# Second FFN of a diffusion layer on one Trainium2 core: a written-out order of steps and units, weight tiles that change places, and some moved mixer passes

## The chip, the cores and the metric

The kernel runs on one core of one Trainium2 chip. The metric is the device time of one execution in microseconds (us). The kernel before takes 2628.71 us, the median of three runs (2627.99 to 2629.0). Its profile is one further execution of 2632.15 us, whose instructions span 2630.2 us.

## The reference

The reference computes one layer of a flow-matching backbone on 256 latent tokens and 256 context tokens of width 2048, all in float32:

```
mod = (silu(c) @ w_mod + b_mod)              # 9 vectors: shift, scale, gate of 3 sub-layers
x  = half_step_ffn(x, mod 0..2, w_ffn1)      # latent and context tokens
h  = rms_norm(x) * (1 + scale) + shift       # adaLN
x += gate * mixer(h)                         # 8 attention heads beside 8 mLSTM heads, then w_out
x  = half_step_ffn(x, mod 6..8, w_ffn2)      # latent tokens alone
out = rms_norm(x, g_final)

def half_step_ffn(x, ...):                   # D_FF = 5632
    a, b = split(adaln(x) @ w_up)
    return x + 0.5 * gate * ((silu(a) * b) @ w_down)
```

## The kernel before

The kernel goes through the first FFN (to about 1320 us), the mixer (to about 1920 us) and the second FFN. Every float32 weight tile arrives by DMA as 128 x 2048 values (1 MB) and is *split* by halves (`split`, lines 118 to 133): ScalarE writes a rounded `hi` half of 1024 columns (L125), VectorE the rest `lo` (L126), and TensorE multiplies three times for each block of 128 rows (`mm3`, L147 to L149). There are four `hi` and four `lo` halves in all, so the splits can run about one tile ahead of TensorE. A framework gives each engine an order of its own from the program's order and its dependencies, and sets the waits; each engine then works through its queue in order. SP's queue issues the plain loads, GpSimd's queue (POOL) issues the loads that add to what a tile holds already (`accum`, L728).

**Second FFN.** The hidden width of 5632 is cut into 11 blocks `n` of 512 columns. Block 0 is made from products prepared in the mixer. Blocks 3 and 10 are made plainly (`up`, two token halves by all of w_up). Blocks 1, 2 and 4 to 9 (`QUADS`) are made by `quad`, which gets the up products of a block with seven products of quarter size in place of eight, from sums of weight tiles and sums of token quarters. A quad is a list `order` of seven blocks (a11, a12, n1, s4, s2, s3, a22) of two steps (`q` = 0, 1) each; a step splits one weight tile and runs 12 matmuls into the accumulators X or Y. The weights of these blocks are sums: two *chained* tiles `chain_` are loaded (`again`, L2114), taken in block a11, then added to in place by `accum` loads; two *third* tiles `ra` are loaded (L2123, at block a12), used in block s4, and enter the chained tile by four half sums on VectorE (`summed_half`, L2073, at the places in `between`); block a12 uses *plain* tiles of the three-deep `raw` pool. After each block a function `use` (`p1`, `c11`, `kept`, `p35`, `c12`, `c22`, `c21`) reads the accumulator, forms Silu(a) * b and puts the product into a list `turn`. `turned()` takes the next one from it, transposes it on TensorE (L2052) and splits the result into `hid2h` and `hid2l` (L2055, L2057); three blocks of these can be held (`N_HID`).

The plain work is a list of *units*: 8 of up(3), 8 each of down(0,1), down(2,3), down(4,5), 8 of up(10) and 8 of down(6,7); a unit loads a tile, splits it and runs 24 matmuls. The last loop of `tile_layer` takes the 48 units in turn and after each as many of the 112 steps of the quads as an even share asks for (two or three). down(8,9), block 10 and the final norm follow. The token quarters' differences (`token_forms`: n1, s2, s4, s3) are made on VectorE beside the first units, in scratch from the `ra` tiles.

**Mixer.** Beside its projections, 128 passes over w_mod run on VectorE (`Beside`, L205), paced by the table `PACE`: pairs of a step count and the number of passes due by then. `N_EARLY` and `N_MIXER` say how many passes may use scratch that other tiles take later. `state` (from L1411) transposes the keys of an mLSTM head on TensorE (L1416), copies them (L1418), and weights the values in four ScalarE instructions (L1422) for the product at L1426. `attention` takes a row maximum (L1684), an exponential on ScalarE (L1688), a reciprocal (L1689), scales the row on ScalarE (L1690), and transposes it on TensorE (L1696).

Of the kernel before, what the change touches and what calls it, by code (L numbers as in the profile page):

```python
# [19 lines left out]
P = 128  # L20
# [16 lines left out]

PACE = (4, 2), (12, 13), (19, 19), (27, 28), (35, 37), (41, 44), (49, 51), (56, 54), (62, 61), (67, 70), (70, 76), (71, 85), (76, 96)
PACE += (83, 102), (87, 109), (91, 118), (94, 130), (97, 144), (101, 152), (107, 163), (110, 170), (128, 181)

# [16 lines left out]
def tile_layer(ctx: ExitStack, tc: tile.TileContext, I: dict, out: bass.AP):  # L57
# [1194 lines left out]
    with ExitStack() as mx:  # L1252
# [30 lines left out]
        mm2 = mm2cm.__enter__()  # L1283
        N_EARLY, N_MIXER = 62, 109

# [126 lines left out]
        def state(h, kTc):  # L1412

            tb = tbank()
            for t in range(2):
                nc.tensor.transpose(tb[:, t * P : (t + 1) * P], kTc[:, t * P : (t + 1) * P], ident)  # L1416
            kn = m1.tile([P, 2, P], F32, tag="kn", name="kn", bufs=1)
            nc.scalar.activation(kn, tb[:, :256].rearrange("p (t d) -> p t d", t=2), AF.Copy)  # L1418
            vw = m1.tile([P, 2, 2, 130], F32, tag="E", name="vw")
            for t in range(2):  # L1420
                for d in range(2):
                    nc.scalar.activation(vw[:, t, d, :], v1[CTX][t][:, h, :], AF.Copy, scale=wg[:, t, d, h : h + 1])  # L1422
            yield
            b = bank()
            for t in range(2):
                nc.tensor.matmul(b[:, :260], kn[:, t, :], vw[:, t, :, :], start=t == 0, stop=t == 1)  # L1426
            nc.scalar.activation(C1[:, h, :, :], b[:, :260].rearrange("p (d c) -> p d c", d=2), AF.Copy)
            yield
# [245 lines left out]
        def attention(kv):  # L1674
            items = [(t, g) for t in range(2) for g in range(4)]
            pr, pT, o = {}, {}, {}
            for i in range(len(items) + 2):
                if i < len(items):
                    t, g = items[i]
                    b = bank()  # L1680
                    qs = [x[:, g, t * P : (t + 1) * P] for x in queries(kv)]
                    mm3(b.rearrange("p (a k) -> p a k", a=2), *qs, *keys[kv], True, True)
                    nm = sm.tile([P, 1], F32, tag="nm", name="nm")
                    nc.vector.tensor_reduce(nm, b, axis=AX.X, op=ALU.max)  # L1684
                    nc.vector.tensor_scalar(nm, nm, -ISQ, None, op0=ALU.mult)
# [3 lines left out]
                    nc.vector.reciprocal(sd, sd)  # L1689
                    nc.scalar.activation(p, p, AF.Copy, scale=sd)  # L1690
                    pr[i] = p
# [234 lines left out]
    with f2x:  # L1926
# [50 lines left out]
        acc2 = f2b.tile([P, 2, D], F32, name="acc2", bufs=1)  # L1977
        chain_ = [f3.tile([P, 2048], F32, tag=f"c{q}", name=f"chain2{q}") for q in range(2)]

# [7 lines left out]
        for q in range(2):  # L1987
            nc.sync.dma_start(chain_[q], part(QUADS[0], 0, q))

# [4 lines left out]
        n1, s4, s2, s3 = ([x[:, 0], x[:, 1]] for x in (forms2[g] for g in ("n1", "s4", "s2", "s3")))  # L1994

        def ra_tile():
            return f2b.tile([P, 2048], F32, tag="ra", name="ra")

        def token_forms():
# [20 lines left out]

            v = ra_tile()[:, :1024].rearrange("p (k c) -> p k c", k=8)
            difference(v, a22, a21)
# [7 lines left out]
            yield  # L2030
            v = ra_tile()[:, :1024].rearrange("p (k c) -> p k c", k=8)
            difference(v, a11, a21)
# [4 lines left out]
        turn = []  # L2037
        summed = set()

        def turned():  # L2040

            if not turn:
                return
            n, t, sa, sign = turn[0]
            if n not in hids:
                if n - 1 not in hids or len(hids) - len(summed) >= N_HID:
                    return
                hids[n] = hid_tiles()
# [15 lines left out]
        def wait_turn(n, t, sa, sign):  # L2064
            turn.append((n, t, sa, sign))
            turn.sort(key=lambda x: x[:2])

# [3 lines left out]
        def quad(n):  # L2071

            add = lambda o, x, y: nc.vector.tensor_tensor(o, x, y, op=ALU.add)  # L2073
            mul = lambda o, x, y: nc.vector.tensor_tensor(o, x, y, op=ALU.mult)
            B, ra, g = {}, {}, {}

# [55 lines left out]
            held = lambda q: chain_[q]  # L2132
            order = (
                (a11, held, "X", True, chained(1, 0), p1),
                (a12, plain, "Y", True, ahead, c11),
                (n1, held, "Y", True, None, kept),
                (s4, lambda q: ra[q], "Y", False, None, p35),
                (s2, held, "X", False, chained(0, 2), c12),
                (s3, lambda q: ra[q], "X", False, None, c22),
                (a22, held, "Y", True, again, c21),  # L2140
            )
            for m, (a, src, dst, fresh, then, use) in enumerate(order):
                for q in range(2):
                    if q == 0 and fresh:
                        B[dst] = psx.tile([P, 512], F32, tag=dst, name=dst)
                    wt = split(src(q))
                    if then:
                        then(q)
                    if (m, q) in between:
                        summed_half(*between[m, q])  # L2150
# [70 lines left out]

        N_UNITS, N_FIRST = 2 * 8 + 4 * 8, 2

# [10 lines left out]
        forms = token_forms()  # L2234
        side, n_side, n_quads = quads(), 0, 14 * len(QUADS)
# [7 lines left out]
        assert u == N_UNITS - 1 and n_side == n_quads  # L2243
        drain(side)
        while turn:
            turned()
        before_final()
# [155 lines left out]
```

## Time and profile before

| what | us |
|---|---|
| median of three runs | 2628.71 |
| profiled execution, its own time | 2632.15 |
| its span, first to last instruction | 2630.2 |
| TensorE matmuls busy (98%) | 2584.3 |
| VectorE busy (82%) | 2159.7 |
| ScalarE busy (55%) | 1433.9 |
| GpSimd busy (8%) | 216.2 |

Busy times of different engines overlap, and so do matmuls, whose ends are modelled. In the tables of waits, "PE tr L2052 <- DVE ca L2074" reads: TensorE, about to transpose on line 2052, stood idle until VectorE had written `ca` on line 2074. PE is TensorE, PEld its weight loads, DVE VectorE, ACT ScalarE, POOL GpSimd, SP the engine that issues the plain loads.

### The profile page before, as it was taken

How to read it: one execution, taken by the hardware profiler on the slowest of the kernel's cores; microseconds unless marked ns; L12 is line 12 of the kernel's file. 1: busy time of each engine (PE TensorE's matmuls, PEld its weight loads, DVE VectorE, ACT ScalarE, POOL GpSimd, SP SyncE). 2: the span in 40 equal slices, each digit the busy share in tenths (PEclk: the TensorE clock that was granted, in tenths of full speed). 3: DMA queues.
4: the chain of work that ended last, by engine and by line, in shares of the span. 5: the costliest groups of instructions: out<-in, count | busy, mean ns of one | idle time of the engine just before them, and what ended most of it. 6: DMA issues, size and time to landing. Idle time of an engine off the chain costs nothing.

```text
span 2630.2 us, 33776 instructions
## 1 busy us (share of the span) xinstructions
PE 2584.3 (98%) x12670; PEld 2142.3 (81%) x12670; DVE 2159.7 (82%) x2832; ACT 1433.9 (55%) x1846; POOL 216.2 (8%) x269
## 2 busy tenths in 40 slices
PE   8999999999999999999999999999999999999998
PEld 5788888888888888888889889878897777777776
DVE  7788888878888788888887889888898878887887
ACT  4454444454454565444463466566576666666663
POOL 0000010100010110001210000220000000000001
PEclk8999999999999999999999999999999999999999
DMA  9989999999999989889977877677678878889876
GB/s 392 354 212 265 284 266 282 255 274 284 281 261 291 262 240 234 226 228 219 229 232 276 315 256 266 220 255 275 238 259 270 254 225 245 248 273 273 245 223 172
DMA packets 127220, 681.01 MB, mean 259 GB/s; under 512 B 14153, under 2 KB 16713, under 8 KB 64977
## 3 DMA queue, kind: packets, MB, share of 16 engines
q1 hardware_dynamic: 98544, 493.25, 50.0%
q0 software_dynamic: 28512, 185.61, 36.1%
q8 instruction: 99, 1.62, 0.2%
q14 instruction: 65, 0.52, 0.1%
HBM read 660.91 MB, written 17.89 MB: 258 GB/s over the span
## 4 chain that ended last, share of the span: by engine, by line
PE 81%; DMA 7%; DVE 6%; issue 3%; ACT 2%; POOL 0%; SPq 0%; ACTq 0%; POOLq 0%; DVEq 0%
PE mm L148 21%; PE mm L149 21%; PE mm L147 20%; DVE lo L126 3%; PE mm L85 2%; DMA chain<-in_w_up2b 2%; PE Y L147 2%; PE Y L148 1%; PE Y L149 1%; ACT hi L125 1%; DMA mraw<-in_w_m 1%; PE tr L148 1%; PE tr L149 1%; PE tr L147 1%; PE X L149 1%
## 5 line engine op out<-in xcount | busy, mean ns | idle before, releaser
L125 ACT ACTIVATE hi<-raw 128x1024 fp32r<-128x1024 f32 (+2 forms) x500 | 517.2, 1040 | 441.8 <-PE mm L149 278.4
L126 DVE TENSOR_TENSOR lo<-raw,hi 128x1024 fp32r<-128x1024 f32 (+2 forms) x488 | 584.4, 1207 | 176.5 <-ACT hi L125 153.7
L125 ACT ACTIVATE hi<-chain 128x1024 fp32r<-128x1024 f32 x368 | 388.1, 1059 | 325.8 <-PE mm L149 185.4
L126 DVE TENSOR_TENSOR lo<-chain,hi 128x1024 fp32r<-128x1024 f32 x368 | 445.4, 1221 | 139.8 <-ACT hi L125 136.1
L147 PE MATMUL mm<-hi,hhi 128*128 128x512 f32 (+3 forms) x1024 | 394.5, 385 | 0.0
L148 PE MATMUL mm<-lo,hhi 128*128 128x512 f32 (+3 forms) x1024 | 387.7, 379 | 0.0
L149 PE MATMUL mm<-hi,hlo 128*128 128x512 f32 (+3 forms) x1024 | 387.4, 378 | 0.0
L205 DVE SCALAR_TENSOR_TENSOR junk<-sraw,cBh 128x1024 fp8e5<-128x1024 f32 x192 | 234.3, 1221 | 22.8 <-DMA sraw<-in_w_mt 20.5
L149 PEld LDWEIGHTS mm<-hi,hlo 128*128 128x128 f32 x1024 | 192.9, 188 | 33.9
L147 PEld LDWEIGHTS mm<-hi,hhi 128*128 128x128 f32 x1024 | 192.9, 188 | 31.4
L148 PEld LDWEIGHTS mm<-lo,hhi 128*128 128x128 f32 x1024 | 193.2, 189 | 30.8
L148 PE MATMUL mm<-lo,hid2h 128*128 128x512 f32 x352 | 138.0, 392 | 2.6 <-DVE lo L126 2.5
L147 PE MATMUL mm<-hi,hid2h 128*128 128x512 f32 x352 | 136.7, 392 | 1.1 <-ACT hi L125 1.1
L149 PE MATMUL mm<-hi,hid2l 128*128 128x512 f32 x352 | 137.2, 390 | 0.0
L205 DVE SCALAR_TENSOR_TENSOR sr<-sr,cBl 128x1024 f32<-128x1024 f32 x85 | 102.5, 1216 | 14.9 <-DMA sr<-in_w_mt 14.8
L728 POOL DMA_DIRECT2D chain<-in_w_up1b x60 | 53.0, 884 | 725.9 <-DVE lo L126 700.5
L147 PE MATMUL mm<-hhi,hi 128*128 128x512 f32 (+1 forms) x288 | 101.2, 351 | 0.0
L148 PE MATMUL mm<-hlo,hi 128*128 128x512 f32 (+1 forms) x288 | 98.9, 343 | 0.0
L149 PE MATMUL mm<-hhi,lo 128*128 128x512 f32 (+1 forms) x288 | 98.9, 343 | 0.0
L125 ACT ACTIVATE hi<-ra 128x1024 fp32r<-128x1024 f32 x64 | 67.9, 1061 | 53.6 <-PE mm L149 31.7
L126 DVE TENSOR_TENSOR lo<-ra,hi 128x1024 fp32r<-128x1024 f32 x64 | 77.5, 1222 | 21.1 <-ACT hi L125 19.6
L148 PEld LDWEIGHTS mm<-lo,hid2h 128*128 128x128 f32 x352 | 66.1, 188 | 18.5 <-DVE lo L126 5.1
(515 smaller groups left out, 5665.6 us busy)
## 6 DMA issues: line engine op xcount, KB each, us to landing
raw<-in_w_dn SPq DMA_DIRECT2D x70, 1024.0 KB, 7.8
chain<-in_w_up1b POOLq DMA_DIRECT2D x60, 1024.0 KB, 10.4
sraw<-in_w_mt SPq DMA_DIRECT2D x96, 512.0 KB, 8.4
sr<-in_w_mt SPq DMA_DIRECT2D x82, 512.0 KB, 5.4
raw<-in_w_up1b SPq DMA_DIRECT2D x40, 1024.0 KB, 8.4
mraw<-in_w_m SPq DMA_DIRECT2D x32, 1024.0 KB, 7.6
raw<-in_w_up2b SPq DMA_DIRECT2D x32, 1024.0 KB, 8.1
chain<-in_w_up2b POOLq DMA_DIRECT2D x32, 1024.0 KB, 11.0
```

Source lines behind the costliest of these rows:

```text
L85: ins = getattr(self.engine, name)(*a, **k)
L125: scalar[0].activation(hi, src, AF.Copy)
L126: vector[0].tensor_tensor(lo, src, hi.bitcast(F32), op=ALU.subtract)
L147: tensor[0].matmul(out_ap, sh, mh, start=first, stop=False, skip_group_check=skip)
L148: tensor[0].matmul(out_ap, sh, ml, start=False, stop=False, skip_group_check=skip)
L149: tensor[0].matmul(out_ap, sl, mh, start=False, stop=last, skip_group_check=skip)
L205: ins = nc.vector.scalar_tensor_tensor(junk() if junk else raw, raw, 1.0, cB[s], op0=ALU.mult, op1=ALU.mult, accum_out=mT[:, i, s, kt, h : ...
L728: accum = lambda dst, src: nc.gpsimd.dma_start(dst, src, accum_op=ALU.add)
```

## The change

1. The last loop no longer shares out steps by a count. A generator `sequence` writes the order: two units, and then for each quad two steps, and six times two steps and a unit (no unit after the fourth block in the last quad of each four).
2. `turned()` takes a product only when two further places of that order (`N_TURN`, counted by `clock`) have gone by since it was formed.
3. The chained and third tiles are two pairs, `weights`, that change roles with each quad. The next quad's first load goes into the third pair at block s3, not into the chained pair at block a22. The third tiles are loaded at block a11 instead of a12.
4. The half sums are put ahead of or behind other splits (`early`, `late_`); each sum and load stays once per quad.
5. The token forms use part of `acc2` as scratch.
6. In the mixer: the table `PACE`, `N_EARLY` (62 to 65) and `N_MIXER` (109 to 111) bring passes forward; in `state` the weighted values come before the transposes, and two of the four move to VectorE; in `attention` the scaling of the row moves to VectorE.

```diff
+N_TURN = 2
-PACE = (4, 2), (12, 13), (19, 19), (27, 28), (35, 37), (41, 44), (49, 51), (56, 54), (62, 61), (67, 70), (70, 76), (71, 85), (76, 96)
-PACE += (83, 102), (87, 109), (91, 118), (94, 130), (97, 144), (101, 152), (107, 163), (110, 170), (128, 181)
+PACE = (4, 2), (12, 13), (19, 19), (27, 28), (35, 37), (42, 44), (51, 51), (58, 54), (65, 61), (70, 70), (73, 76), (74, 85), (79, 96)
+PACE += (86, 102), (92, 109), (98, 118), (100, 130), (103, 144), (106, 152), (109, 163), (112, 170), (128, 181)
...
+            vw = m1.tile([P, 2, 2, 130], F32, tag="E", name="vw")
+            for d in range(2):
+                nc.scalar.activation(vw[:, 0, d, :], v1[CTX][0][:, h, :], AF.Copy, scale=wg[:, 0, d, h : h + 1])
+                nc.vector.tensor_scalar(vw[:, 1, d, :], v1[CTX][1][:, h, :], wg[:, 1, d, h : h + 1], None, op0=ALU.mult)
...
-                    nc.scalar.activation(p, p, AF.Copy, scale=sd)
+                    nc.vector.tensor_scalar(p, p, sd, None, op0=ALU.mult)
...
+            if clock[0] < born[n, t] + N_TURN:
+                return
...
+            i = QUADS.index(n)
+            chain_, ra = weights[i % 2], weights[1 - i % 2]
+
             def again(q):
                 if n != QUADS[-1]:
-                    nc.sync.dma_start(chain_[q], part(QUADS[QUADS.index(n) + 1], 0, q))
+                    nc.sync.dma_start(ra[q], part(QUADS[i + 1], 0, q))
...
-            def ahead(q):
-                ra[q] = ra_tile()
+            def first(q):
+                accum(chain_[q], part(n, 1, q))
                 nc.sync.dma_start(ra[q], part(n, 1, 2 + q))
...
-                if h:
-                    accum(ra[q], part(n, 1, q))
-
-            between = {(2, 1): (0, 0), (3, 0): (0, 1), (3, 1): (1, 0), (4, 0): (1, 1)}
+
+            def early(m, q):
+                if (m, q) == (3, 0):
+                    summed_half(0, 1)
+                elif (m, q) == (4, 0):
+                    summed_half(1, 1)
+                    accum(ra[1], part(n, 1, 1))
+
+            def late_(m, q):
+                if (m, q) == (2, 1):
+                    summed_half(0, 0)
+                elif (m, q) == (3, 0):
+                    accum(ra[0], part(n, 1, 0))
+                elif (m, q) == (3, 1):
+                    summed_half(1, 0)
...
-                (a11, held, "X", True, chained(1, 0), p1),
-                (a12, plain, "Y", True, ahead, c11),
+                (a11, held, "X", True, first, p1),
+                (a12, plain, "Y", True, None, c11),
...
-                (s3, lambda q: ra[q], "X", False, None, c22),
-                (a22, held, "Y", True, again, c21),
+                (s3, lambda q: ra[q], "X", False, again, c22),
+                (a22, held, "Y", True, None, c21),
...
+        def sequence():
+
+            yield from "uu"
+            for n in range(len(QUADS)):
+                yield from "ss"
+                for m in range(1, 7):
+                    yield from "ss"
+                    if m != 3 or n % 4 != 3:
+                        yield "u"
...
-        for u, _ in enumerate(units()):
-            steps(forms)
+        streams = {"u": units(), "s": quads()}
+        for x in sequence():
+            next(streams[x])
+            if x == "u":
+                steps(forms)
+            clock[0] += 1
             turned()
-            while n_side < n_quads * (u + 1 - N_FIRST) / (N_UNITS - N_FIRST):
-                next(side)
-                n_side += 1
-                turned()
```

More of the change, by code (lines that the diff above doesn't have):

```diff
@@ L1283, in tile_layer @@
         mm2 = mm2cm.__enter__()
-        N_EARLY, N_MIXER = 62, 109
+        N_EARLY, N_MIXER = 65, 111
         early2 = one([P, 2, 1024], "early2", tag="mqT")
@@ L1418, in state @@
             nc.scalar.activation(kn, tb[:, :256].rearrange("p (t d) -> p t d", t=2), AF.Copy)
[L1419 to L1422, printed above, removed]
             yield
@@ L1977, in tile_layer @@
         acc2 = f2b.tile([P, 2, D], F32, name="acc2", bufs=1)
-        chain_ = [f3.tile([P, 2048], F32, tag=f"c{q}", name=f"chain2{q}") for q in range(2)]
+        weights = [[f3.tile([P, 2048], F32, tag=f"c{q}", name=f"chain2{q}") for q in range(2)]]
+        weights.append([f2b.tile([P, 2048], F32, name=f"ra{q}", bufs=1) for q in range(2)])
         LAST = NF // FB - 1
@@ L1987, in tile_layer @@
         for q in range(2):
-            nc.sync.dma_start(chain_[q], part(QUADS[0], 0, q))
+            nc.sync.dma_start(weights[0][q], part(QUADS[0], 0, q))
         hv = [x.rearrange("p k (t c) -> p t k c", t=2) for x in (h2hi[:, :, :T], h2lo[:, :, :T])]
@@ L1994, in tile_layer @@
         n1, s4, s2, s3 = ([x[:, 0], x[:, 1]] for x in (forms2[g] for g in ("n1", "s4", "s2", "s3")))
-        def ra_tile():
-            return f2b.tile([P, 2048], F32, tag="ra", name="ra")
         def token_forms():
@@ L2019, in negative_less @@
                 sub(v, v, l)
-            v = ra_tile()[:, :1024].rearrange("p (k c) -> p k c", k=8)
+            v = acc2[:, 0, :1024].rearrange("p (k c) -> p k c", k=8)
             difference(v, a22, a21)
@@ L2030, in token_forms @@
             yield
-            v = ra_tile()[:, :1024].rearrange("p (k c) -> p k c", k=8)
+            v = acc2[:, 0, 1024:].rearrange("p (k c) -> p k c", k=8)
             difference(v, a11, a21)
@@ L2038, in tile_layer @@
         summed = set()
+        born, clock = {}, [0]
         def turned():
@@ L2065, in wait_turn @@
             turn.append((n, t, sa, sign))
+            born[n, t] = clock[0]
             turn.sort(key=lambda x: x[:2])
@@ L2074, in quad @@
             mul = lambda o, x, y: nc.vector.tensor_tensor(o, x, y, op=ALU.mult)
-            B, ra, g = {}, {}, {}
+            B, g = {}, {}
             def p1():
@@ L2145, in quad @@
                         B[dst] = psx.tile([P, 512], F32, tag=dst, name=dst)
+                    early(m, q)
                     wt = split(src(q))
@@ L2148, in quad @@
                         then(q)
-                    if (m, q) in between:
-                        summed_half(*between[m, q])
+                    late_(m, q)
                     for j in range(4):
@@ L2220, in units @@
             yield from down(6, 7)
-        N_UNITS, N_FIRST = 2 * 8 + 4 * 8, 2
+        def sequence():
[6 more added lines that the diff above has]
+                        yield "u"
         def before_final():
@@ L2234, in tile_layer @@
         forms = token_forms()
-        side, n_side, n_quads = quads(), 0, 14 * len(QUADS)
-        for u, _ in enumerate(units()):
-            steps(forms)
-            turned()
-            while n_side < n_quads * (u + 1 - N_FIRST) / (N_UNITS - N_FIRST):
-                next(side)
-                n_side += 1
-                turned()
-        assert u == N_UNITS - 1 and n_side == n_quads
-        drain(side)
+        streams = {"u": units(), "s": quads()}
[4 more added lines that the diff above has]
+            clock[0] += 1
+            turned()
+        for x in streams.values():
+            assert next(x, x) is x
         while turn:
+            clock[0] += 1
             turned()
```

## The prediction

> **What bounds the kernel now.** I read the page first, then a table of stages, then the table of TensorE's waits in the last stage, and only then the timeline around single waits. The stage table (busy us of each engine in each stretch, granted clock, DMA share):
>
> ```profile
> span 2630.2 us, 33776 instructions
> ```
>
> ```profile
> core 0: us, PE busy (x) PEld busy (x) DVE busy (x) ACT busy (x) POOL busy (x), PEclk, DMA share, GB/s
> 400.00:1000.00 600.00, 600.00 (x2702) 495.89 (x2701) 494.45 (x616) 308.08 (x355) 54.64 (x62) 1.00 0.97 270
> 1735.00:1835.00 100.00, 97.04 (x519) 80.78 (x518) 82.97 (x148) 71.17 (x110) 6.51 (x6) 0.98 0.75 267
> 1950.00:2600.00 650.00, 630.79 (x2779) 510.47 (x2778) 517.68 (x492) 398.91 (x422) 47.08 (x54) 1.00 0.85 251
> ```
>
> TensorE is the bound: in the first FFN (400 to 1000) it is never idle. In the second FFN (1950 to 2600) it is idle for 650.0 - 630.8 = 19.2 us, and that is the pool from which the main edit can win. Who ended those waits, by the table of waits of that stretch (us in total, times, longest):
>
> ```profile
> PE tr L2052 <- DVE ca L2074: 6.5, 6, 1.8
> PE mm L148 <- DVE lo L126: 3.8, 6, 0.8
> PE mm L147 <- ACT hi L125: 2.5, 4, 0.8
> PE Y L147 <- DVE ca L2073: 2.2, 3, 0.9
> PE Y L147 <- ACT cy L2087: 2.1, 6, 0.7
> PE X L148 <- DVE lo L126: 1.9, 3, 0.7
> ```
>
> A wait costs more than its idle figure. Two places of TensorE's timeline (start, duration, idle before it in brackets):
>
> ```profile
> 2163.74 0.69 PE L147 MATMUL mm<-hi,hid2h 128*128 128x512 f32 x2
> 2165.10 0.50 PE L148 MATMUL mm<-lo,hid2h 128*128 128x512 f32 x1 [0.68 <-DVE lo L126]
> 2165.43 0.39 PE L149 MATMUL mm<-hi,hid2l 128*128 128x512 f32 x1
> 2165.67 0.39 PE L147 MATMUL mm<-hi,hid2h 128*128 128x512 f32 x1
> ...
> 2184.09 0.39 PE L149 MATMUL mm<-hi,hid2l 128*128 128x512 f32 x1
> 2186.30 0.63 PE L2052 MATMUL tr<-ident,ca 128*128 128x128 f32 x4 [1.82 <-DVE ca L2074]
> ```
>
> Undisturbed matmuls start 0.23 us apart but last 0.39, so 0.16 of each stall is booked as busy (2184.09 to 2186.30 is 2.21, of which 1.98 is lost and 1.82 shown). The first matmul after a wait also takes 0.33 to the next start, 0.10 more. The six rows hold 28 waits and 19.0 us: 6 before transposes lose 6.5 + 6 x 0.16 = 7.5 us, the other 22 lose 12.5 + 22 x 0.26 = 18.2. **Pool: 25.7 us.**
>
> Why VectorE and ScalarE are late there:
>
> ```profile
> ACT hi L125 <- DMA chain<-in_w_up2b: 26.8, 13, 3.9
> ...
> ```
>
> ```profile
> 1950.00:1997.00 47.00, 45.04 (x198) 36.38 (x197) 46.52 (x43) 30.48 (x33) 2.70 (x3) 1.00 0.79 265
> ...
> 2147.00:2222.00 75.00, 71.75 (x315) 57.59 (x314) 60.05 (x59) 45.32 (x48) 5.22 (x6) 1.00 0.84 251
> ```
>
> ScalarE waits 13 times for a chained tile to land. VectorE is busy 60 of 75 us in a typical quad but 46.5 of the first 47 us, where it also makes the token forms.
>
> **The change part by part.** *Fixed order.* A quad has 14 steps of 12 matmuls (2.7 us each) and takes 6 units of 24 matmuls (5.4 us). Before, a counter puts a unit after every second or third step, wherever that falls; TensorE's built order cuts blocks in two and even units ("2 matmuls of a unit, 12 of Y, 22 of the unit"). After, a unit stands behind every block of two steps but the first, so whole blocks of 24 alternate. Every accumulator that a block reuses has then a unit of 5.4 us in which VectorE or ScalarE may read it: the Y waits (2.2 + 2.1 us idle, 9 times) end. No instruction is added; the work of a quad is 14 x 12 + 6 x 24 matmuls on both sides.
>
> VectorE's load per block and unit. Its rows (mean ns) and its back-to-back pace:
>
> ```profile
> L126 DVE TENSOR_TENSOR lo<-chain,hi 128x1024 fp32r<-128x1024 f32 x368 | 445.4, 1221 | 139.8 <-ACT hi L125 136.1
> ...
> L2073 DVE TENSOR_TENSOR chain<-chain,ra 128x1024 f32<-128x1024 f32 x32 | 38.4, 1219 | 0.2
> ```
>
> ```profile
> 1980.84 2.35 DVE L126 TENSOR_TENSOR lo<-chain,hi 128x1024 fp32r<-128x1024 f32 x2
> 1983.11 1.22 DVE L2001 TENSOR_TENSOR s3f<-ra,s3f 128x1024 fp32r<-128x1024 f32 x1
> ```
>
> Two splits start 2.27 apart, so I count 1.14 each (and 0.6 for a 512-wide add of 0.68). Block plus unit needs 6 splits = 6.8 us against 10.9 us of TensorE. The fullest pair (n1) adds two half sums (2.3), one add (0.6) and, in half of the cases, two additions to the output (1.2): 10.9 against 10.9, with the buffers' lead of one step (2.7) as reserve. The two blocks without a unit between them need 9.1 + 1.2 + 0.6 = 10.9 against 10.9, after a unit that needs 2.3 of 5.4. So ordinary quads stall little: I take 1 us for all (0 to 8, the upper end being one wait of about 1 us per quad). The first quad still carries token forms; in the built order of VectorE s4, s3 (15 passes of the four forms in all, 17 us) fall among the half sums of blocks n1 and s4. Walking that queue with 1.14 per pass, from the start of the first unit (the forms begin 0.5 later), five halves come late, in us ready / wanted: the first plain tile's second half 18.0 / 17.7, the unit after n1 33.5 / 33.0, the two tiles of s4 39.3 / 39.0 and 42.6 / 42.0, the unit after s4 46.0 / 45.2. Together 0.3 + 0.5 + 0.3 + 0.6 + 0.8 = 2.5, with resumes 3 us (2 to 6); before, 1.96 us idle there. Where the cover of a unit is gone (blocks s4 and s2 of every fourth quad) VectorE has only splits to do.
>
> *Late turn.* A product may be transposed two places after it is formed, so 5.4 us or more of matmuls lie between the last matmul of a block and its transposes. Add, Silu and product need about 0.7 + 0.6 + 0.7 plus two splits in VectorE's queue, 4.3 us. The 7.5 us go; what is late next is the second half of the hidden block, first read two blocks later, so nothing. At the end 16 transposes instead of 8 stand together before the last products: 0.5 us lost (0 to 1.5).
>
> *Tiles change places.* The next quad's first load goes into the third tile at s3 rather than into the chained tile at a22: 4 steps and 2 units of lead, 21.7 us, in place of 2 steps and at most a unit or two. On SP's queue it stands between the two plain tiles, and waits for splits that are done in that same order, so it holds nothing up. The third tile's load now follows the previous a22. Landing times in the stage:
>
> ```profile
> q0 software_dynamic: 7485, 49.81, 42.3%
> q1 hardware_dynamic: 13894, 101.20, 41.7%
> ...
> chain<-in_w_up2b POOLq DMA_DIRECT2D x30, 1024.0 KB, 11.4
> ...
> chain<-in_w_up2b SPq DMA_DIRECT2D x14, 1024.0 KB, 6.8
> ```
>
> 21.7 covers 6.8 three times, so these ScalarE waits go. Accumulating loads at s4, s2 have 4 steps and 2 units too. The first ones (block a11 to block n1) have 4 steps and one unit, 16.3 us from start to start; less 1.4 (the second half of the split may be that late) and 2.3 (one hi and one lo ahead of the matmul) leaves **12.6 us**, up to 15 where the split ran a step ahead, against the median 11.4. Bandwidth: 84% of 610 us for some 8 quads is 63 us per quad; in 71.5 us that is 0.88, and the first FFN ran 0.97 without a wait.
>
> Sum for the stage: 25.7 - 1 - 3 - 0.5 = **21.2 us** won. The acc2 scratch for the forms adds nothing: nothing else uses it yet.
>
> *Mixer.* Scaling of the attention rows goes from ScalarE to VectorE, half of the weighted values too, and the paced passes come up to 7 places earlier (128 passes on both sides, hidden beside TensorE, as VectorE has 17% idle; a pass without that cover costs 1.14).
>
> ```profile
> PE tr L1696 <- ACT pr L1690: 3.0, 2, 2.1
> ...
> PE tr L1416 <- ACT cy L1458: 0.6, 1, 0.6
> PE mm L1426 <- ACT kn L1418: 0.5, 1, 0.5
> ```
>
> ```profile
> L1690 ACT ACTIVATE pr<-pr,sd 128x512 f32<-128x512 f32 x16 | 11.5, 718 | 5.5 <-DVE sd L1689 5.4
> ...
> L1422 ACT ACTIVATE vw<-v1c,wg 128x130 f32<-128x130 f32 x32 | 10.1, 395 | 0.1
> ```
>
> ```profile
> L2281 DVE TENSOR_SCALAR acc<-acc,rstd 128x512 f32<-128x512 f32 x3 | 1.4, 484 | 0.7 <-POOL rstd L2274 0.7
> ...
> L1909 DVE TENSOR_SCALAR rr<-ones,rstd 128x128 f32<-128x128 f32 x2 | 0.6, 288 | 1.4 <-POOL rstd L155 1.4
> ```
>
> VectorE gets 16 x 0.48 + 16 x 0.29 = 12.4 us, ScalarE loses 11.5 + 6.3. The shown waits are 4.1 us; a shorter path by 0.2 and one hand-over less takes part of them. Bounds: all 4.1 plus the slow clock below (5.8 won), or 5 us lost if VectorE (83% busy) becomes late for splits. I take 2 us won, near the waits' rows.
>
> ```profile
> 1745.03 1.23 DVE L205 SCALAR_TENSOR_TENSOR sr<-sr,cBl 128x1024 f32<-128x1024 f32 x1 [0.52 <-DMA sr<-in_w_mt]
> ...
> 1748.28 0.66 PE L1696 MATMUL tr<-ident,pr 128*128 128x128 f32 x4 [2.07 <-ACT pr L1690]
> ...
> 1749.36 0.66 PE L147 MATMUL mm<-hi,hhi 128*128 128x512 f32 x1
> 1749.82 0.63 PE L148 MATMUL mm<-lo,hhi 128*128 128x512 f32 x1
> ```
>
> After the idle 2.07 us matmuls start 0.46 apart, and the granted clock of that stretch is 0.98: 0.02 x 100 us is some 2 us of lost clock. [...] In my sum the clock stands only as the upper bound.
>
> Sum: 2632.15 (the profiled execution's own time) - 21.2 - 2 = 2609. The median of the runs shown, 2628.71, lies 3.4 below that execution, so **2606 us** is predicted.
>
> **Rivals.** (1) *The chained tile lands late, moderately.* For: third-tile loads may now stand beside the first accumulating loads, 4 MB within two steps. Against: SP issues them behind the a22 splits, a unit earlier. Landing at about 14 us instead of 11.4 costs 1.5 us in each of 8 quads: 2606 + 12 = 2618. [...]
>
> (2) *The same transfer, slower than before.* All landings of the chained tile in the stage:
>
> ```profile
> DMA to landing us min/median/max: 5.5/9.3/17.3
> ```
>
> If each quad met the longest, 17.3 - 12.6 = 4.7 us would be lost in block n1, 8 times: 2606 + 38 = 2644. It ends slower once a landing passes 12.6 + 23/8 = 15.5. For: 17.3 does occur. Against: it occurs where four accumulating loads follow each other, which the first pair does not meet.
>
> (3) *VectorE becomes late in the mixer:* the 5 us above in place of 2 won: 2613.
>
> (4) *The waits only move:* every block of two steps waits for VectorE's half sums as long as before; about 2629. Against: VectorE has 20% idle in the quads.
>
> **Chances.** Forecast 0.60, (1) 0.17, (2) 0.06, (3) 0.10, (4) 0.07. Range: below, the whole pool and the mixer's bound, 2632.15 - 25.7 - 4.5 - 3.4 = 2599; above, rival (1), 2619. A measurement tells about 0.2% (5 us) from no change. Faster 0.87, same 0.07, slower 0.06.
>
> **What would show it.** Right: in the second FFN TensorE idles 3 to 6 us instead of 19.2, no row of transposes waiting for ca, no ScalarE wait for chained loads at a11, remaining waits in the first quad. Wrong: waits of hi for the chained tile at n1 (rivals 1, 2); a new row of transposes or matmuls waiting for VectorE's pr or lo between 1461 and 1835 (rival 3).

## The result, and the profile after

The changed kernel takes 2604.93 us (median of four runs, 2603.34 to 2609.73), the kernel before, timed beside it, 2628.59 us (2627.99 to 2629.0). The ratio is 0.9913 with a 95% interval of 0.9896 to 0.993: 23.7 us faster. The profiled execution took 2604.58 us.

The stage table of the changed kernel (columns as before; the last stretch ends at 2573, where block 10 and the last products begin to run out):

```profile
span 2602.7 us, 33781 instructions
```

```profile
1735.00:1835.00 100.00, 97.31 (x525) 80.93 (x523) 83.84 (x151) 57.45 (x91) 10.38 (x10) 1.00 0.67 228
1950.00:2573.00 623.00, 622.19 (x2775) 512.91 (x2774) 519.71 (x493) 403.60 (x422) 47.21 (x54) 1.00 0.88 261
```

In the second FFN TensorE is idle for 623.0 - 622.2 = 0.8 us, where it was 19.2. Its table of waits there has three rows left, one wait each, and all three lie in the first quad:

```profile
PE Y L150 <- DVE lo L128: 0.3, 1, 0.3
PE mm L150 <- DVE lo L128: 0.3, 1, 0.3
PE Y L149 <- ACT cy L2091: 0.2, 1, 0.2
```

No transpose waits for `ca` any more. ScalarE's waits for loads of the chained tiles in that stretch (26.8 us, 13 times, before) are down to three; the pairs change roles, so the same load bears the name chain in one quad and ra in the next:

```profile
ACT hi L127 <- DMA chain<-in_w_up2b: 4.3, 2, 3.5
...
ACT hi L127 <- DMA ra<-in_w_up2b: 2.2, 1, 2.2
```

In the mixer the longest wait has only changed the engine that ends it: it was ScalarE's `pr`, it is VectorE's, and is as long as before.

```profile
PE tr L1698 <- DVE pr L1692: 2.8, 2, 2.1
...
PE tr L1422 <- ACT cy L1460: 0.7, 1, 0.7
```

**Where the time came from** is seen best by cutting each trace at two instructions of TensorE: the first matmul that reads `h2hi` (the products prepared for block 0, in the last 20 us of the mixer) and the last matmul of all. From TensorE's timeline, the kernel before, then the changed one:

```profile
1901.06 0.37 PE L442 MATMUL mm<-h2hi,hi 128*128 128x258 f32 x1
...
2619.75 0.39 PE L149 MATMUL mm<-hi,hid2l 128*128 128x512 f32 x1
```

```profile
1900.58 0.37 PE L444 MATMUL mm<-h2hi,hi 128*128 128x258 f32 x1
...
2592.97 0.39 PE L151 MATMUL mm<-hi,hid2l 128*128 128x512 f32 x1
```

The stage shrinks from 2619.75 - 1901.06 = 718.7 us to 2592.97 - 1900.58 = 692.4 us, 26.3 us. Everything ahead of it differs by 0.5 us, the tail behind it by 0.7. So in this pair of traces the whole gain is in the second FFN, and the mixer's edits gave about nothing; ffn_only and mixer_only, below, test that.

### The profile page after: what moved, and what is told of

Its sections match the earlier page's. It is cut to its first block, busy times and chain, and to the rows that moved or that the text cites. A ratio compares the mean times of both kernels' runs of the same rounds, so it can differ in the third digit from the quotient of the medians.

```text
span 2602.7 us, 33781 instructions
## 1 busy us (share of the span) xinstructions
PE 2575.7 (99%) x12670; PEld 2144.7 (82%) x12670; DVE 2170.6 (83%) x2864; ACT 1417.7 (54%) x1810; POOL 220.7 (8%) x269
## 4 chain that ended last, share of the span: by engine, by line
PE 85%; DVE 7%; DMA 5%; issue 2%; ACT 1%; POOL 0%; ACTq 0%; POOLq 0%; SPq 0%; DVEq 0%
PE mm L151 21%; PE mm L150 21%; PE mm L149 21%; DVE lo L128 2%; PE mm L87 2%; PE Y L149 2%; PE Y L151 2%; PE Y L150 2%; PE X L151 2%; PE X L150 2%; PE X L149 2%; PE tr L150 1%; PE tr L149 1%; PE tr L151 1%; PE tr L87 1%
## 5 line engine op out<-in xcount | busy, mean ns | idle before, releaser
L127 ACT ACTIVATE hi<-chain 128x1024 fp32r<-128x1024 f32 x336 | 355.0, 1059 | 305.7 <-PE mm L151 188.0
L128 DVE TENSOR_TENSOR lo<-chain,hi 128x1024 fp32r<-128x1024 f32 x336 | 407.2, 1221 | 118.0 <-ACT hi L127 114.3
L207 DVE SCALAR_TENSOR_TENSOR junk<-sraw,cBh 128x1024 fp8e5<-128x1024 f32 x192 | 234.3, 1220 | 19.2 <-DMA sraw<-in_w_mt 16.7
L128 DVE TENSOR_TENSOR lo<-ra,hi 128x1024 fp32r<-128x1024 f32 x96 | 117.0, 1223 | 39.7 <-ACT hi L127 35.8
L127 ACT ACTIVATE hi<-ra 128x1024 fp32r<-128x1024 f32 x96 | 101.9, 1061 | 65.1 <-PE mm L151 48.4
L149 PE MATMUL mm<-hi,sumshl 128*128 128x512 f32 x200 | 77.8, 389 | 0.0
```

The costliest lines, as they stand in the source:

```text
L127: scalar[0].activation(hi, src, AF.Copy)
L128: vector[0].tensor_tensor(lo, src, hi.bitcast(F32), op=ALU.subtract)
L149: tensor[0].matmul(out_ap, sh, mh, start=first, stop=False, skip_group_check=skip)
L207: ins = nc.vector.scalar_tensor_tensor(junk() if junk else raw, raw, 1.0, cB[s], op0=ALU.mult, op1=ALU.mult, accum_out=mT[:, i, s, kt, h : ...
```

## The experiments

Three groups of four kernels; the kernel before was timed again beside each group (2632.75, 2631.86 and 2630.83 us), so the ratios compare, not the times. "Stage" is the time between the two matmuls above in the kernel's one trace, "idle" what TensorE idles from 1950 to 2573 (in held_first, whose stage ends 85 us later, this is a smaller part of the work).

| kernel | us | ratio and 95% interval | stage | idle |
|---|---|---|---|---|
| before (first profile) | 2628.59 | 1 | 718.7 | 19.1 |
| order_only | 2615.48 | 0.9933 (0.9921 to 0.9946) | 703.2 | 8.8 |
| tiles_only | 2625.33 | 0.997 (0.9959 to 0.9982) | 707.9 | 10.1 |
| turn_at_once | 2607.27 | 0.9904 (0.9889 to 0.9919) | 692.1 | 0.8 |
| no_swap | 2608.42 | 0.9912 (0.9898 to 0.9925) | 694.9 | 3.8 |
| ffn_only | 2604.06 | 0.9895 (0.9881 to 0.991) | 691.7 | 0.5 |
| mixer_only | 2634.21 | 1.0012 (1.0002 to 1.0021) | 717.2 | 18.7 |
| sums_back | 2608.45 | 0.9908 (0.9893 to 0.9922) | 693.3 | 1.6 |
| late_first | 2605.57 | 0.9895 (0.9879 to 0.9912) | 693.4 | 1.4 |
| turn_only1 | 2631.38 | 0.9999 (0.9989 to 1.0008) | 717.3 | 19.0 |
| held_first | 2693.33 | 1.0236 (1.0219 to 1.0252) | 776.7 | 55.0 |
| best | 2603.08 | 0.9894 (0.9877 to 0.9911) | 691.2 | 0.5 |
| after_again | 2604.42 | 0.9902 (0.9886 to 0.9917) | 691.5 | 0.5 |

The stage is the sharper measure: kernels whose second FFN is that of before lie at 717.2 to 718.7 (mean 717.7), those with the changed one at 691.2 to 692.4 (mean 691.7), while the time ahead of it scatters from 1898.9 to 1907.2 over all these traces (1900.6 and 1907.0 for the very same changed kernel).

### Which part won: the second FFN or the mixer

ffn_only is the changed kernel with the mixer's lines as before; mixer_only is the kernel before with the mixer's lines changed:

```diff
-                    nc.vector.tensor_scalar(p, p, sd, None, op0=ALU.mult)
+                    nc.scalar.activation(p, p, AF.Copy, scale=sd)
... (and PACE, N_EARLY, N_MIXER, vw as before)
```

> The changed kernel with the mixer as before (pace, state, attention). Theory: the mixer edits are worth what the two traces show, waits of 4.1 us idle before against about 4.6 after, so nothing or at most 1 us: 2604 to 2607. Rival (the prediction's term): 2 us, 2607; or the mixer edits cost and this is faster, 2602.

> The kernel before with the mixer edits alone. Theory: within 1 us of the kernel before, 2628. Rival (the prediction's term): 2626.5; rival (VectorE late): 2633.

ffn_only is as fast as the changed kernel, as its theory had it. mixer_only wins nothing, it is slower by 0.5 to 5.5 us: 1.0012 (1.0002 to 1.0021). So of the three expectations for it the rival with VectorE late is nearest, though the interval is wide. Its wait stands at the same place with the same length, now ended by VectorE:

```profile
PE tr L1696 <- DVE pr L1690: 3.2, 2, 2.1
```

Beside it stand two rows of transposes that wait for VectorE (L1604, 0.6 us each). Rows of this kind, 0.8 to 2.3 us together, are in every trace with the mixer's edits and in none without them.

### Order or tiles

order_only puts the written-out sequence into the kernel before and nothing else. tiles_only is the changed kernel with the old share-out by a count and no late turn; the change of roles, the sums' places, the scratch and the mixer's edits stay.

```diff
 order_only (from before)
+        streams = {"u": units(), "s": quads()}
+        for x in sequence():
+            next(streams[x])
+            if x == "u":
+                steps(forms)
             turned()
-            while n_side < n_quads * (u + 1 - N_FIRST) / (N_UNITS - N_FIRST):
...
 tiles_only (from after)
-N_TURN = 2
+N_TURN = 0
+            while n_side < n_quads * (u + 1 - N_FIRST) / (N_UNITS - N_FIRST):
...
```

> The kernel before with the written-out order of steps and units alone (turn at once, old tile roles, old places of the half sums, old mixer). Theory (each of the three FFN edits removes its own waits): the Y waits and most split waits go, the waits of transposes for ca (6.5 us idle) stay, and the chained tile reloaded at a22 has 2 steps and 1 unit, 10.9 us, less 3.7 of lead, so 7 us against landings of 7 to 9: about 1 us of TensorE lost per quad. TensorE idle 10 to 12 us in the second FFN instead of 19.2, time about 2615. Rival A (the order does it all): idle under 2 us, 2606. Rival B (the exchange of the tiles does it): idle over 15, about 2623.

> The changed kernel with the old sharing-out of steps and turn at once: exchange of tiles, new places of the half sums and the mixer edits stay. Theory: ScalarE's waits for chained tiles at a11 go, Y waits and waits of transposes stay: TensorE idle 12 to 15 us in the second FFN, time about 2620. Rival A (order does it all): idle about 19, 2627. Rival B (tiles do it): idle under 6, about 2610.

Against the 717.7 us of the old stage order_only wins 14.5 and tiles_only 9.8; together 24.3, against 26.0 for the whole change. The two are close to additive, and take away different waits. The theory for order_only held, with a little less idle time (8.8 us) than it had. That for tiles_only held in time (2620 expected is 0.997 of before) but not in its reason: the transposes' waits, which it expected to stay, went. TensorE's waits of order_only:

```profile
PE tr L2052 <- DVE ca L2074: 4.4, 4, 3.0
PE X L147 <- ACT s3f L2006: 3.7, 1, 3.7
```

and of tiles_only:

```profile
PE mm L150 <- DVE lo L128: 4.1, 7, 0.8
PE Y L149 <- DVE ca L2077: 2.7, 4, 0.9
PE Y L149 <- ACT cy L2091: 2.1, 6, 0.7
```

The fixed order ends the waits of Y and of `lo`, which tiles_only still has. The tiles end the transposes' waits, which order_only still has, without any late turn. order_only's second row is the s3 form of the first quad: its scratch is a tile of the `ra` pool, and it comes some 25 us later in the stage than in the changed kernel, where the scratch is `acc2`. ScalarE's timeline of order_only, then of the changed kernel:

```profile
2015.52 1.06 ACT L2006 ACTIVATE s3f<-ra 128x1024 fp32r<-128x1024 f32 x1 [1.52 <-DVE ra L2001]
```

```profile
1988.31 1.06 ACT L2006 ACTIVATE s3f<-acc 128x1024 fp32r<-128x1024 f32 x1 [0.76 <-DVE acc L2001]
```

The 3.7 us wait has a second price: behind it the granted clock is 0.50 for 3.4 us, another 1.7 us. The scratch alone was not tried. Every kernel with it in `acc2` lacks that row; but so does the kernel before, which has its scratch in `ra` too and makes this form at 1981.73, ahead of the third tiles' use. So it is that scratch together with the written-out order that is late.

### Why the transposes waited

The prediction had the late turn remove these waits. The rival: the Silu that `ca` needs stands in ScalarE's queue behind a `hi` split that waits for a chained tile to land. ScalarE's timeline of the kernel before around the transposes at 2263 us (which wait 1.5 us):

```profile
2258.24 2.01 ACT L125 ACTIVATE hi<-chain 128x1024 fp32r<-128x1024 f32 x2 [2.72 <-DMA chain<-in_w_up2b]
...
2261.19 0.63 ACT L2105 ACTIVATE ca<-ca 128x512 f32<-128x512 f32 x1 [0.95 <-DVE ca L2073]
...
2263.70 0.60 ACT L2055 ACTIVATE hid2h<-tr 128x512 fp32r<-128x512 f32 x1 [1.88 <-PE tr L2052]
```

The two `hi` halves start 2.7 us late, and the Silu of L2105 (its operand from VectorE, 0.95 us late, hangs on the `lo` of the same tile in VectorE's queue) follows them. That is no single case: each of the six waits of transposes in this trace ends 3.1 to 4.8 us after such a late split of a chained tile began, and so do the four of order_only (4.8 us each). Three kernels tell the two apart: turn_at_once (the changed kernel without the late turn), turn_only1 (the kernel before with a late turn of one place, half of the changed kernel's two; as I read the code, with two the old share-out would reach a hidden block before it is transposed), and no_swap (the changed kernel, late turn and all, but with fixed roles, the next quad's first load at a22 again).

```diff
 turn_at_once
-N_TURN = 2
+N_TURN = 0
 turn_only1 (from before)
+N_TURN = 1
+            if clock[0] < born[n, t] + N_TURN:
+                return
 no_swap
-            chain_, ra = weights[i % 2], weights[1 - i % 2]
+            chain_, ra = weights
...
-                    nc.sync.dma_start(ra[q], part(QUADS[i + 1], 0, q))
+                    nc.sync.dma_start(chain_[q], part(QUADS[i + 1], 0, q))
```

> The changed kernel with N_TURN 0, so that a product may be transposed as soon as it is in the list. Theory: the transposes wait for ca again, 16 turns of which some 6 to 10 wait 1 us: TensorE idle 6 to 9 us in the second FFN, time 2605 + 7 = 2612. Rival: in the fixed order the framework finds a better place for the transposes by itself, idle under 2 us, 2605.

> The changed kernel with fixed roles: the next quad's first load goes into the chained tile again, at a22. Theory: that load has 2 steps and a unit of lead (about 7 us net) against a landing of 7 to 9, ScalarE waits for it at a11 in most quads, TensorE loses about 1 us in each of 7 quads: idle 5 to 8 us, time about 2612. Rival: VectorE's and ScalarE's lead of one tile hides it, idle under 2 us, 2605.

> The kernel before with the late turn alone (one place of the sequence, N_TURN = 1). Theory (transposes wait because ScalarE, which works in order, has the Silu of that block behind a hi split that waits for the chained tile's load): most of the transposes' waits stay, TensorE idles at least 15 of the 19.2 us in the second FFN, the time is 2626 to 2631, ratio 0.999 to 1.001. Rival (the prediction's step: a later turn removes them): no row of transposes waiting for ca, idle about 12.5, 7 us faster, ratio about 0.997.

turn_at_once has the whole gain (stage 692.1), turn_only1 none of it (717.3), and no_swap keeps two waits of transposes in spite of the late turn. The waits go with the loads, in all three, and in tiles_only, which has the loads early, the product turned at once and no such wait. The theory of turn_at_once (transposes wait again, 7 us lost) failed, that of turn_only1 held. turn_only1's row, and the load row beside it:

```profile
PE tr L2057 <- DVE ca L2080: 6.3, 6, 1.6
...
ACT hi L127 <- DMA chain<-in_w_up2b: 20.9, 10, 3.7
```

and no_swap's:

```profile
PE tr L2055 <- DVE ca L2078: 3.3, 2, 1.7
...
ACT hi L127 <- DMA chain<-in_w_up2b: 18.2, 9, 4.1
```

ScalarE still waits 18.2 us in no_swap, and the stage is only 3.2 us longer by it: the fixed order leaves most of these waits covered. The theory for no_swap (about 1 us lost in each of seven quads) was too dark: two quads lost it.

### The leads of the loads

sums_back puts the half sums and the third tile's accumulating loads to their old places. late_first moves the line of the first accumulating load from block a11 to block a12. held_first does that in earnest: GpSimd first reads one column of the plain tile's `lo`, with a small operation whose result nobody uses, and only then issues the load.

```diff
 sums_back
-                    early(m, q)
...
-                    late_(m, q)
+                    if (m, q) in between:
+                        summed_half(*between[m, q])
 late_first
-                accum(chain_[q], part(n, 1, q))
...
-                (a12, plain, "Y", True, None, c11),
+                (a12, plain, "Y", True, chained(1, 0), c11),
 held_first
-                accum(chain_[q], part(n, 1, q))
...
+                    if m == 1:
+                        seen = sm.tile([P, 1], F32, tag="nm", name="seen")
+                        pin(nc.gpsimd.tensor_scalar(seen, wt(slice(CB * 3, CB * 3 + 1))[1].bitcast(F32), 1.0, 0.0, op0=ALU.mult, op1=ALU.add))
+                        pin(accum(chain_[q], part(n, 1, q)))
```

> The changed kernel with the half sums at the places of the kernel before (after their step's split) and each third tile's accumulating load after both its sums. Theory: the built order of VectorE moves the sums anyway and a unit stands beside each pair, so TensorE idle stays under 2.5 us: 2605 to 2607. Rival (their place matters): a wait of about 1 us per quad, 2613.

> The changed kernel with the first accumulating load of each chained tile one block later (at a12 instead of a11), so with 2 steps and a unit of lead instead of 4 steps and a unit: net 12.6 - 5.4 = 7.2 us, up to 9.6 where the split ran ahead, against landings of 8 to 12. Theory (landing beyond the net lead stops TensorE at block n1, the point of rivals 1 and 2): hi at n1 waits for the chained tile in nearly every quad, TensorE loses 1 to 3 us in each of 8 quads, 2613 to 2629. Rival (the lead has more slack than was counted): under 0.5 us per quad, 2605 to 2609.

> The changed kernel; before each first accumulating load GpSimd reads one column of the lo half of the block after a11 (a small operation whose result nobody uses), so the two loads into the chained tiles are issued one block, about 5.4 us, later: net lead 7 us in place of 12.5, against landings of 8 to 10. Theory (the lead of this load is what the kernel lives on, rival 1 of the prediction): ScalarE waits for the chained tile before block n1 in nearly every quad and TensorE stalls there, 1 to 2 us a quad: 2613 to 2621, ratio 0.994 to 0.997. Rival (the splits run far enough ahead that 5 us less of lead are absorbed): under 0.5 us a quad, within 4 us of the changed kernel, ratio 0.990 to 0.993.

sums_back costs some 1.6 us of stage, hardly more than the scatter; its theory held. late_first tests nothing: GpSimd's queue holds few other things, its issue waits only for the `lo` of a11, and so happens at the same time with the line at either place (131.6 us into the stage in the changed kernel, 132.1 here, in the second quad). held_first really moves it. In the changed kernel's second quad GpSimd issues the two loads and ScalarE takes the first of the tiles (it comes under the name ra in this quad):

```profile
2032.16 0.86 POOL L730 DMA_DIRECT2D ra<-in_w_up2b  x1 [26.93 <-DVE lo L128]
...
2037.29 0.88 POOL L730 DMA_DIRECT2D ra<-in_w_up2b  x1 [4.26 <-DVE lo L128]
...
2044.53 1.06 ACT L127 ACTIVATE hi<-ra 128x1024 fp32r<-128x1024 f32 x1 [0.30 <-PE Y L151]
```

The lead (from the issue to the start of the split) is 12.4 us, and ScalarE is held by a buffer that TensorE still reads, not by the load. In held_first:

```profile
2054.13 1.25 POOL L2170 TENSOR_SCALAR seen<-lo 128x1 f32<-128x1 f32 x1 [34.98 <-DVE lo L128]
2055.33 0.89 POOL L730 DMA_DIRECT2D ra<-in_w_up2b  x1
...
2058.30 0.91 POOL L730 DMA_DIRECT2D ra<-in_w_up2b  x1
```

```profile
2067.41 2.00 ACT L127 ACTIVATE hi<-ra 128x1024 fp32r<-128x1024 f32 x2 [9.26 <-DMA ra<-in_w_up2b]
...
2074.73 2.00 ACT L127 ACTIVATE hi<-ra 128x1024 fp32r<-128x1024 f32 x2 [4.80 <-DMA ra<-in_w_up2b]
```

ScalarE wants the first tile at 2067.41 - 9.26 = 2058.2: 2.8 us after its issue, where I meant to leave 7. In the changed kernel the same moment, when ScalarE is free for the split, lies 12.1 us after the issue; so the hold took 9.3 us of lead, not 5.4. The small operation itself is 1.25 us of that; the rest is how far the awaited `lo` lies behind a11's in VectorE's queue. And the two loads, now 3 us apart, are there only 12 and 16 us after their issue. TensorE pays in each quad:

```profile
PE Y L149 <- ACT hi L127: 42.3, 15, 7.0
PE Y L150 <- DVE lo L128: 12.1, 19, 0.8
```

```profile
1950.00:2573.00 623.00, 567.95 (x2404) 455.71 (x2403) 457.25 (x429) 352.03 (x376) 57.21 (x60) 0.96 0.77 230
```

The stage grows by 776.7 - 691.7 = 85.0 us, 10.6 a quad, and the kernel is slower than before, 1.0236 (1.0219 to 1.0252). Up to 2573 the idle time is 55 us; a granted clock of 0.96 is another 0.04 x 623 = 25: behind the 7.04 us wait that ends at 1986.95 and the 3.31 us wait that ends at 2068.52, for example, matmuls start 0.43 us apart in place of 0.23. Theory and rival both missed: my expected 1 to 2 us a quad had neither the real lead nor the clock.

### A version that might beat both

best is ffn_only with two pairs of the pacing table changed and one added. A pair (n, s) holds pass n back until step s (the first number counts passes, the second steps; the description of the kernel before has them the other way round). The aim is that no pass over w_mod stands on VectorE between the maximum and the reciprocal of the second and third attention row. after_again is the changed kernel once more, beside it.

```diff
-PACE += ... (97, 144), (101, 152), (107, 163), ...
+PACE += ... (98, 144), (99, 154), (103, 158), (107, 163), ...
```

> The second FFN's edits with the mixer as it was, and four pairs of the table that paces the passes shifted so that no pass stands in VectorE's queue between the row maximum and the reciprocal of the second and third attention row. Theory (the 2.1 us wait of the attention's transposes stays because paced passes and a split stand on VectorE inside that chain): that wait falls to 1 us or less, 1 to 3 us faster than the changed kernel, ratio 0.989 to 0.990. Rival (the passes only bunch later and another wait takes its place): same time as the changed kernel within 1 us, ratio 0.990 to 0.992, and the mixer's idle time of TensorE stays at 5 us or more.

> The changed kernel itself beside the other three: 2605 us, ratio 0.990 to 0.992, TensorE idle under 1.5 us in the second FFN. Both theories expect the same; it is the yardstick for differences of a few us.

Why the attention's wait stayed is on VectorE's timeline of the changed kernel, one row maximum to its scaled row:

```profile
1743.23 0.68 DVE L1686 TENSOR_REDUCE nm<-mm 128x1 f32<-128x512 f32 x1
1743.83 1.21 DVE L207 SCALAR_TENSOR_TENSOR sr<-sr,cBl 128x1024 f32<-128x1024 f32 x1
...
1745.03 1.21 DVE L207 SCALAR_TENSOR_TENSOR sr<-sr,cBl 128x1024 f32<-128x1024 f32 x1
...
1746.17 1.22 DVE L128 TENSOR_TENSOR lo<-raw,hi 128x1024 fp32r<-128x1024 f32 x1
1747.31 0.15 DVE L1691 RECIPROCAL sd<-sd 128x1 f32<-128x1 f32 x1
1747.50 0.49 DVE L1692 TENSOR_SCALAR pr<-pr,sd 128x512 f32<-128x512 f32 x1
```

Two passes and a split, 3.5 us, stand between the maximum and the reciprocal; the scaling behind them, 0.49 in place of 0.72, is a small part. In best nothing stands between the maximum of that row (1742.33) and its reciprocal (1744.11) but a 0.15 us operation; behind the next row's maximum (1746.20) a split and one pass still do. The longest of these waits is 0.9 in place of 2.1:

```profile
PE tr L1698 <- ACT pr L1692: 2.3, 3, 0.9
```

The sum of that row falls only from 3.0 (ffn_only) to 2.3, and 2603.08 us cannot be told from the 2604.42 beside it (0.9894, 0.9877 to 0.9911, and 0.9902, 0.9886 to 0.9917). The wait fell as theory had it; a faster kernel is not shown.

## Why the prediction was right, and where its steps failed

- **Pool: right in place and nearly in size.** The second FFN held 25.7 us by the count of waits; the stage shrank by 26.3 (24.8 to 27.5 over the pairs of traces). That is some 2 us more than the pool less what is left of it (25.7 - 1.6), so the hidden part of a wait was counted a little small, or it is the scatter of about 1 us.
- **What was kept back, 1 + 3 + 0.5: too much.** The three waits that are left show 0.8 us, with 0.26 each for the hidden part and the resume 1.6, all in the first quad. Ordinary quads have none. The transposes that gather at the end cost nothing that shows: with and without the late turn the stage is 692.4 and 692.1. The second FFN was sized at 21.2 won and gave 26.3 in the profiles, and the sign of "3 to 6 us" idle was missed on the good side, 0.8.
- **Late turn: the wrong cause.** "The 7.5 us go" holds, but not by the late turn. "Add, Silu and product need about 0.7 + 0.6 + 0.7 plus two splits in VectorE's queue" left out ScalarE's queue, where the Silu stood behind a split that waited for a load. The late turn itself is worth no more than the scatter (stage 692.1 without it, 691.2 to 692.4 with it). The pool was right because it had been counted from TensorE's waits, whatever took them away.
- **Tiles change places: right.** The waits of ScalarE for the chained tile went from 26.8 to 6.5 us. The step put no time of its own on it; alone it is worth 3.2 us of stage (no_swap), and more, 9.8 with sums and scratch, where the order is uneven (tiles_only).
- **"The acc2 scratch for the forms adds nothing": wrong by the look of order_only,** where the s3 form in an `ra` tile comes some 25 us later and costs 3.7 us in one wait and 1.7 of clock. With the written-out order the scratch matters; by itself it was not tried.
- **Fixed order: right.** The Y waits end, and VectorE keeps up. It is the largest single part, 14.5 us of stage, even with the s3 wait in it.
- **Rivals 1 and 2: the mechanism exists, the case occurred once, and cheaply.** The lead of the first accumulating loads, 12.6 by the sum, is 12.4 in the trace. In the first quad one of them takes 12.1 us to land: ScalarE waits 3.5 us for it at block n1 (1976.87); TensorE has no wait in that block, its three lie later, from 1983 to 1996. From the second quad on they land within 7.9 to 10.1 us, and ScalarE never waits for them. The 11.4 that the sum used is a median over all accumulating loads into the chained tiles; the slow ones, up to 17.4, belong to the last pair of a quad, where four follow each other, as the prediction said against rival 2. Shortened to 2.8 the kernel is slower than before, at a price well above the one I gave, because the loads then land later (12 and 16 us after their issue in the second quad) and the slow clock (0.96 granted) comes on top.
- **Mixer, 2 us won: failed.** The step read the wait as the scaling's engine and its hand-over; it is the queue of VectorE in front of the reciprocal. The passes brought forward and the moved values gave nothing either. Rival 3 did show its sign (a row waiting for VectorE's `pr`), as a wait that took the place of the old one, with 0.8 to 2.3 us of other waits for VectorE; mixer_only is 0.5 to 5.5 us slower, so rival 3's 5 us are at the edge of what is measured.
- **The forecast's total** was closer than its steps. Between the two profiled executions the sum was 4.4 us short (2609 against 2604.58). Most of that is hidden because before's profiled execution lay 3.4 above its median and was corrected for it, while the changed kernel's lies 0.4 below its own. That 2606 came within 1.1 us of the median is in part luck: the second FFN gave 5.1 us more than its term, the mixer at least 2 less.
- **Small slips in the sums:** the lower end of the range uses 4.5 us for the mixer, where the part on the mixer has 5.8 (2597 instead of 2599); 84% of 610 us over 8 quads is 64 us, not 63. Neither changes the forecast.

The time ahead of the second FFN differs by 6.4 us between the two traces of the changed kernel. Most of that can be placed: one wait of the mixer near 1492 us is 2.4 us in after_again and 0.7 in the first profile, and after_again has two half-rate stretches, at 1494.0 and 1753.4, of some 1.6 us each, which the first profile does not have. About 1.5 us stay open.

## What to carry to other kernels

Count a pool of stalls from the bound engine's waits, but do not name what removes each from the releaser's row alone: follow the releaser back through its own queue, where something older may be waiting for a load. The lead of a load is to be reckoned from its issue to the split, which runs ahead of the matmul; here 9 us less of it made a kernel slower than before out of one that did not wait. And cut the traces at two instructions of the bound engine: here a stage's length repeated to about 1 us where whole executions of the changed kernel scattered by 7 (2602.8 to 2610.0).

## What the runs showed of the hardware

**The same wait, with and without a slow clock.** The attention's wait of 2.07 to 2.15 us occurs in nearly every trace. In the kernel before matmuls ran at half rate behind it (0.43 us apart). In the changed kernel they do not (0.31, then 0.23):

```profile
1748.13 0.63 PE L1698 MATMUL tr<-ident,pr 128*128 128x128 f32 x4 [2.14 <-DVE pr L1692]
...
1749.41 0.47 PE L149 MATMUL mm<-hi,hhi 128*128 128x512 f32 x1
1749.72 0.39 PE L150 MATMUL mm<-lo,hhi 128*128 128x512 f32 x1
```

and in ffn_only they do again, 0.43 apart for some 3 us, in place of 0.23:

```profile
1746.68 0.66 PE L1698 MATMUL tr<-ident,pr 128*128 128x128 f32 x4 [2.15 <-ACT pr L1692]
...
1748.38 0.63 PE L150 MATMUL mm<-lo,hhi 128*128 128x512 f32 x1
1748.81 0.63 PE L151 MATMUL mm<-hi,hlo 128*128 128x512 f32 x1
...
1751.27 0.39 PE L151 MATMUL mm<-hi,hlo 128*128 128x512 f32 x1
```

All traces but that of best have this wait. Nine of the thirteen have one stretch of 3.41 us at a granted clock of 0.50 at its end or within 1.3 us behind it, and four have none (the changed kernel, order_only, no_swap, late_first); over 1735 to 1835 the granted clock is 0.98 in the kernel before and 1.00 in the changed kernel and in order_only. The same 22 intervals between matmuls after the wait take 3.6 to 3.9 us without the stretch and 5.2 to 5.5 with it: 1.6 us. order_only, with the wait of before, has none, so the change is not what ended it.

What decides between the two cases is left open here. The wait's length alone does not: in the kernel before it is 2.07 us (1746.21 to 1748.28), and the granted clock from 1749.5 to 1752.9 is 0.50; in the changed kernel it is 2.14 us (1745.99 to 1748.13), and the granted clock from 1746.8 to 1753.6 is 1.00:

```profile
1749.50:1752.90 3.40, 3.40 (x10) 2.63 (x10) 1.16 (x3) 1.66 (x4) 0.00 (x0) 0.50 0.97 337
```

```profile
1746.80:1750.20 3.40, 2.07 (x16) 1.97 (x17) 3.37 (x7) 0.73 (x2) 0.00 (x0) 1.00 0.95 367
1750.20:1753.60 3.40, 3.40 (x16) 2.80 (x15) 1.67 (x5) 1.84 (x3) 0.00 (x0) 1.00 0.81 273
```

So here two waits of about the same length differed in price by 1.6 us.

**Moving the line of a load on GpSimd's queue did not move its issue** in late_first: there and in the changed kernel the issue waits for VectorE's `lo`, 26.94 and 26.93 us.
